# A backbone kernel on one core: first fold group in whole fp32, mod rows gathered, context modulated on VectorE

## The chip, the core and the metric

The kernel runs on one core of a Trainium2 chip. A core has five engines with queues of their own: TensorE (PE in the profile; PEld is its weight load), VectorE (DVE), ScalarE (ACT), GpSimd (POOL) and SyncE (SP), which here issues nearly all DMA transfers. Each engine works through its queue in order; semaphores make it wait for others. The metric is the device time of one execution in microseconds (us). Before the change it is 1301.46 us, the median of three runs (1300.69 to 1303.47).

## What is computed

Two layers over 1024 latent tokens of width 1024, with 256 context tokens. The parts that the change touches are the modulated norms of x and of the context, the context's projection in layer 0, and the weights of layer 1's pooling mixer:

```python
def rmsnorm(x, g):
    y = xf * lax.rsqrt(jnp.mean(xf * xf, axis=-1, keepdims=True) + RMS_EPS)
    return y * g
...
for l in range(DEPTH):
    shift, scale, gate = jnp.split(silu(c) @ mod_w[l] + mod_b[l], 3, axis=-1)
    hx = rmsnorm(x, norm_g[l]) * (1 + scale) + shift
    if l % 2 == 0:
        hc = rmsnorm(ctx, norm_g[l]) * (1 + scale_c) + shift_c
        xb_c = hc @ w_in[:, 3 * W_CONV:3 * W_CONV + W_LRU]
        _, h_ctx = rglru_branch(xb_c, pe, h0, False)
        out_x, _ = even_mixer(hx, h_ctx, pe)
    else:
        out_x = odd_mixer(hx, po, True)
    x = x + gate[:, None] * out_x
```

In the even mixer hx is multiplied by w_in (parts va, vg, ga, xb, gb); xb goes through a short convolution and a gated linear recurrence. In the odd mixer each of four groups of channels is pooled and multiplied by its `w_grp`. The kernel multiplies part of the input weights by `w_grp` beforehand: this product is called the fold.

## The kernel before

Everything is held with channels on the 128 partitions and tokens along the free axis: x in eight tiles of 128x1024 (`x_0` to `x_7`), each the tokens of 128 channels. Matmuls are made exact enough by a split: an fp32 tensor is cast to a high part of type fp32r (names with h: `h0h`, `wh_xb`, `gh`, `cth`) by ACT, and the low part, the difference (`h0l`, `wl_xb`, `gl`, `ctl`), is subtracted by POOL or DVE. Three matmul passes follow, high by high, high by low and low by high (`mm3_steps`, lines 137 to 139).

The first stage lies in `sequence` (lines 522 to 585), before the projections of layer 0 begin. It has these parts.

- **Fold** (`fold_early`, lines 296 to 334). Three groups are done here, with 4, 4 and 2 blocks of `wu`. A block of 128x1024 gives eight products of 128x512 (line 323); ACT copies the two results from PSUM (`fo`, line 328) and they are stored (`wfold`). Only the first block of group 0 is multiplied as whole fp32 (`graw` and `wu`); all others go through the split, line 101 or 106 on ACT, and four subtractions of 256 columns each on POOL (`split_small`, line 108).
- **Factors** (`dots`, line 394). A tile `mod` is multiplied on DVE with the broadcast vector `c` and summed (`junk`, line 397); ACT adds the bias (line 401) or makes the scale (`factor`, line 392). The last channels' factors come from `mod_row` (line 414): 16 matmuls on PE (line 422), a copy of the row by ACT (`modrow`, line 425), and four transposes on PE (line 428), for each of the two rows.
- **Norm of x** (`x_load`, line 459; `x_roots`, line 507). Squares on ACT, added up on POOL and DVE in `ssq`; column sums by PE (`ms_x`, line 512), root on ACT, reciprocal and a diagonal (`dg_x`, line 516) on DVE, and a matmul with ones that spreads the result over all partitions (line 519). `modulate` (line 435) then makes `h0h` and `h0l` of each tile.
- **Context** (`ctx_load`, `ctx_scale`, `ctx_split`, lines 491 to 505). The squares of eight pieces of 256 columns are added by POOL into `ssqc` (line 381); PE sums them over the channels (`ms_c`, line 194), ACT and DVE make the reciprocal root, DVE scales (line 501), POOL modulates eight pieces (line 452), ACT casts and POOL subtracts.
- **First projection** (line 825 on). The weights `xb0` are loaded and split, `wl_xb` on POOL. PE computes `xb` (48 matmuls of 512 columns), the context's `xbc` (24 of 256), `vg`, `va`, and then the gates `g` of the recurrence, which need `uc` (the short convolution of xb and xbc) and u on DVE.

The order on each engine is fixed when the program is built. Within the first stage a scheduler sets it: an instruction goes where its operands and its priority put it, `tc.high_priority` moves a step ahead, and `tc.issue_after` puts it behind another instruction. All loads of the stage form one chain on SP (`load`, line 112), so that they are issued in the order of the code. From the projections on, the order is recorded by `on` (line 595). Tiles come from rings of buffers (`wr`, `wh`, `wl`: two each; `x`: eight; `d`: 16): a new tile waits until the buffer's former one has been read for the last time.

## Time and profile before

| | |
|---|---|
| median of 3 runs | 1301.46 us (1300.69 to 1303.47) |
| profiled execution, its own time | 1300.71 us |
| span of that execution, first to last instruction | 1298.9 us |
| mean granted TensorE clock | 0.994 of full |
| DVE, ACT and POOL busy in the span | 1129.6, 660.2 and 398.5 us |
| data moved | 182.92 MB in 83507 packets |

In the rows of the timeline the columns are the start in us from the span's beginning, the length, the engine, the line, the operation, output<-input, the shape and how many instructions the row gathers; in brackets stands how long the engine was idle before and for whom it waited. In the rows of the windows they are the window, its length, for each engine the busy time and the number of instructions, the granted clock, the share of the DMA engines and GB/s. A row of waits gives who waited for whom, the sum, how often and the longest. A row of the chain that ended last gives start, length and what ran. A matmul in whole fp32 leaves two records, one in fp32r a single one.

### The profile page before, as it was taken

The numbers are of one execution on the slowest core, as the hardware profiler recorded it, in microseconds if no ns is written. First come the engines' busy times: TensorE is split into PE (matmuls) and PEld (weight loads), VectorE is DVE, ScalarE is ACT, GpSimd is POOL, SyncE is SP. The second block draws the span as 40 slices with busy tenths as digits, with TensorE's granted clock in tenths as the row PEclk, the third lists the DMA queues.
The fourth block names the chain that finished last, engine by engine and source line by source line (L and its number), as shares of the span: only waits on it lengthen the run. The fifth ranks groups of instructions, "written<-read, shape, count | busy, mean of one in ns | idle before, by whom it ended". The sixth has DMA issues, their size and how long they took to land.

```text
span 1298.9 us, 16083 instructions
## 1 busy us (share of the span) xinstructions
PE 1267.6 (98%) x5706; PEld 1039.7 (80%) x5706; DVE 1129.6 (87%) x1758; ACT 660.2 (51%) x977; POOL 398.5 (31%) x260
## 2 busy tenths in 40 slices
PE   8988999999999999999999999999999999999997
PEld 5667788888888888888888787888888888778786
DVE  7755999999999999998679868989999986887876
ACT  7663456656665654324635445744434444544543
POOL 4685347664766642353320006000000000000002
PEclk9989999999999999999999999999999999999999
DMA  9973112111221223452464555243343324677723
GB/s 371 326 221 138 49 41 73 51 56 42 73 70 55 68 77 104 140 171 98 137 200 157 188 185 179 90 147 118 111 141 132 122 99 149 228 261 251 283 98 130
DMA packets 83507, 182.92 MB, mean 141 GB/s; under 512 B 8034, under 2 KB 28002, under 8 KB 83428
## 3 DMA queue, kind: packets, MB, share of 16 engines
q1 hardware_dynamic: 76948, 178.75, 40.5%
q10 hardware_dynamic: 6480, 3.15, 0.9%
q8 instruction: 44, 0.72, 0.2%
q14 instruction: 35, 0.29, 0.1%
HBM read 137.84 MB, written 44.04 MB: 140 GB/s over the span
## 4 chain that ended last, share of the span: by engine, by line
PE 82%; DVE 7%; DMA 5%; ACT 3%; issue 1%; POOL 1%; SPq 0%; POOLq 0%; ACTq 0%; DVEq 0%
PE wob L595 7%; PE gb L595 7%; PE vg L595 6%; PE xb L595 6%; PE va L595 6%; PE g L595 4%; PE fold L323 2%; PE fold L595 2%; DMA yr_b<-y_b 2%; PE ga L595 2%; PE ga L139 2%; PE ga L137 2%; PE ga L138 2%; PE qb_v L1083 1%; PE qb_v L1085 1%; PE qb_v L1086 1%
## 5 line engine op out<-in xcount | busy, mean ns | idle before, releaser
L595 DVE SCALAR_TENSOR_TENSOR conv<-u,sm,conv 128x505 f32<-128x505 f32 (+6 forms) x224 | 153.7, 745 | 0.9
L1914 POOL TENSOR_TENSOR o<-x,rr 128x256 f32<-128x256 f32 (+1 forms) x10 | 9.4, 969 | 446.6 <-ACT rr L1850 444.7
L595 POOL TENSOR_TENSOR l<-l,l 128x1280 f32<-128x1280 f32 (+1 forms) x23 | 63.9, 2794 | 91.8 <-DVE l L595 65.6
L595 ACT ACTIVATE l<-g,sm 128x512 f32<-128x512 f32 (+1 forms) x96 | 58.6, 618 | 62.0 <-PE g L595 60.2
L595 PE MATMUL va<-h0h,wl_va 128*128 128x512 f32 x128 | 49.9, 390 | 1.3 <-POOL wl_va L595 1.3
L595 PE MATMUL vg<-h0h,wl_vg 128*128 128x512 f32 x128 | 50.0, 391 | 0.0
L595 PE MATMUL wob<-ybh,wh_wob 128*128 128x512 f32 x128 | 49.9, 390 | 0.0
L595 PE MATMUL vg<-h0h,wh_vg 128*128 128x512 f32 x128 | 49.8, 389 | 0.0
L595 PE MATMUL vg<-h0l,wh_vg 128*128 128x512 f32 x128 | 49.8, 389 | 0.0
L595 PE MATMUL wob<-ybh,wl_wob 128*128 128x512 f32 x128 | 49.8, 389 | 0.0
L595 PE MATMUL gb<-h0l,wh_gb 128*128 128x512 f32 x128 | 49.8, 389 | 0.0
L595 PE MATMUL gb<-h0h,wh_gb 128*128 128x512 f32 x128 | 49.8, 389 | 0.0
L595 PE MATMUL wob<-ybl,wh_wob 128*128 128x512 f32 x128 | 49.8, 389 | 0.0
L595 PE MATMUL va<-h0h,wh_va 128*128 128x512 f32 x128 | 49.8, 389 | 0.0
L595 PE MATMUL gb<-h0h,wl_gb 128*128 128x512 f32 x128 | 49.8, 389 | 0.0
L595 PE MATMUL va<-h0l,wh_va 128*128 128x512 f32 x128 | 49.8, 389 | 0.0
L595 DVE TENSOR_TENSOR_SCAN l<-l,l 128x256 f32<-128x256 f32 (+1 forms) x32 | 48.7, 1521 | 1.1
L101 ACT CAST wq_g<-wr_g 128x512 fp32r<-128x512 f32 x48 | 28.2, 620 | 40.8 <-DMA wr_g<-wg 15.7
L595 POOL TENSOR_TENSOR l<-l,uc 128x1280 f32<-128x1280 f32 x16 | 48.1, 3032 | 0.0
L595 DVE SCALAR_TENSOR_TENSOR conv<-cL,wsum,conv 128x506 f32<-128x506 f32 (+3 forms) x70 | 47.5, 745 | 0.2
L101 ACT CAST wq_wo<-wr_wo 128x512 fp32r<-128x512 f32 x48 | 28.7, 620 | 36.5 <-DMA wr_wo<-wo 17.3
L108 POOL TENSOR_TENSOR wl_wu<-wr_wu,wh_wu 128x256 fp32r<-128x256 f32 x24 | 17.3, 754 | 92.1 <-ACT wh_wu L106 92.1
(667 smaller groups left out, 4413.2 us busy)
## 6 DMA issues: line engine op xcount, KB each, us to landing
mod<-modT SPq DMA_DIRECT2D x20, 512.0 KB, 7.0
x_part<-xp SPq DMA_DIRECT2D x32, 256.0 KB, 3.3
mod<-modT SPq DMA_DIRECT2D x32, 256.0 KB, 3.3
wr_v<-wfold SPq DMA_DIRECT2D x16, 512.0 KB, 3.8
wr_g<-wg SPq DMA_DIRECT2D x16, 512.0 KB, 4.7
wr_wo<-wo SPq DMA_DIRECT2D x16, 512.0 KB, 3.6
y_b<-y SPq DMA_DIRECT2D x24, 256.0 KB, 3.3
y_t<-y SPq DMA_DIRECT2D x24, 256.0 KB, 3.6
```

Source lines behind the costliest of these rows:

```text
L101: return (nc.scalar.copy(hi, src), eng.tensor_tensor(out=lo, in0=src, in1=hi.bitcast(F32), op=sub))
L108: nc.gpsimd.tensor_tensor(out=lo[:, n : n + C], in0=src[:, n : n + C], in1=hi.bitcast(F32)[:, n : n + C], op=sub)
L137: nc.tensor.matmul(ps, hi[:, kc], xh[k][:, cols], start=(k == 0), stop=False)
L138: nc.tensor.matmul(ps, hi[:, kc], xl[k][:, cols], start=False, stop=False)
L139: nc.tensor.matmul(ps, lo[:, kc], xh[k][:, cols], start=False, stop=(k == ks - 1))
L323: nc.tensor.matmul(ps[s], parts[p][0][:, kc], parts[p][1][i], start=(p + i == 0), stop=(p == n - 1 and i == 3))
L595: last[eng] = f(*args, **kw)
L1083: nc.tensor.matmul(ps, hi, xh[k], start=(first and k == 0), stop=False, skip_group_check=not first)
L1085: nc.tensor.matmul(ps, hi, xl[k], start=False, stop=False, skip_group_check=not first)
L1086: mm = nc.tensor.matmul(ps, lo, xh[k], start=False, stop=(k == KH - 1), skip_group_check=not first)
L1914: nc.gpsimd.tensor_tensor(out=outs[k // per][:, k % per], in0=x1[k][:, cols], in1=rr, op=mult)
```

## The change

Nothing of the result changes but the rounding of group 0's fold. The parts are these.

- Group 0 of the fold is multiplied whole: `graw_0_*` and its four `wu` stay fp32, without casts or subtractions, 32 products in place of 8 whole ones and 72 passes. The first loads are now graw, wu, graw, mod (before: mod, graw, graw, wu).
- The ACT steps of the first factors are held back in `small_steps` until the last square of x; `decay_rates` gets a high priority. The last sum for the norm of x is on DVE.
- `mod_row`, called twice, becomes `mod_rows`: all four loads, then 32 matmul records behind the second spread matmul, one copy for both rows, the transposes. Tiles `mod` 1, 9, 2 and 10 are loaded earlier, `mod` 3 later.
- Fold group 1 follows the mod rows; the modulation of x starts earlier in the code.
- The weights `xb0` are loaded and split ahead of the context and of fold group 2. In the queues of PE, group 2 now stands between `xb` and `xbc`.
- The context's squares are added in PSUM (`csum`) by DVE, the sum is spread by one matmul, and DVE multiplies each of the eight pieces by its factor and the reciprocal root in one step and subtracts for the low part; ACT casts in between. POOL does nothing for the context.

The core of the diff:

```diff
-    def fold_early(g, kps, out_tile, g_tile):
+    def fold_early(g, kps, out_tile, g_tile, whole_tile):
         gs, gh, gl = [], [], []
         for i in range(2):
-            raw = (dtile if g < 2 else xtile)(f"graw_{g}_{i}")
+            raw = (whole_tile if g < 2 else xtile)(f"graw_{g}_{i}")
             load(raw, grp[g, i])
-            th, tl = g_tile(i)
-            split_small(raw, th, tl)
-            for t, l in ((raw, gs), (th, gh), (tl, gl)):
-                l += [t[:, h] for h in HALF]
+            if g:
+                th, tl = g_tile(i)
+                split_small(raw, th, tl)
+                for t, l in ((th, gh), (tl, gl)):
+                    l += [t[:, h] for h in HALF]
+            else:
+                gs += [raw[:, h] for h in HALF]
+                if i == 0:
+                    w0 = wpool.tile([P, D], F32, tag="wr", name="wu_0_0")
+                    load(w0, wu[0, 0])
         yield
         for kp in kps:
-            w = (dtile if (g, kp) < (1, 3) else xtile if (g, kp) == (2, 0) else wr_tile)(f"wu_{g}_{kp}")
-            load(w, wu[g, kp])
-            if (g, kp) == (0, 0):
+            if g == 0:
+                w = w0 if kp == 0 else wpool.tile([P, D], F32, tag=("wh", "wl", "wr")[kp - 1], name=f"wu_{g}_{kp}")
+                if kp:
+                    load(w, wu[g, kp])
                 parts = ((w, gs),)
             else:
+                w = (wr_tile if g < 2 else xtile)(f"wu_{g}_{kp}")
+                load(w, wu[g, kp])
                 wh, wl = [wpool.tile([P, D], F32R, tag=t, name=f"{t}_wu_{g}_{kp}") for t in ("wh", "wl")]
-                if (g, kp) == (0, 1):
-                    split(w, wh, wl, nc.vector)
-                else:
-                    split_small(w, wh, wl)
+                split_small(w, wh, wl)
...
             nc.scalar.activation(a0[:, :, k], m0[:, :, KT + k], AF.Identity, scale=col(O_NG + k), bias=bias)
 
-        def dots(m):
+        small_steps = []
+
+        def dots(m, held=False):
...
+            if held:
+                small_steps.append(step)
+            else:
+                step()
...
+        def mod_rows():
+            whole = psum("modr")
+            raws = {}
+            for j in (1, 0):
+                for q in range(KT // KW):
+                    raws[j, q] = dtile(f"modw_{j}_{q}")
+                    load(raws[j, q][:, : KW * KR * P], modW[j, q])
+            for j in (1, 0):
+                ps = whole[:2, j * KR * P : (j + 1) * KR * P]
+                with tc.issue_after(spread[0].ins):
+                    for k in range(KT):
+                        e = k % KW
+                        nc.tensor.matmul(ps, ccv[:, k], raws[j, k // KW][:, e * KR * P : (e + 1) * KR * P],
+                                         start=(k == 0), stop=(k == KT - 1))
+            row = ttile("modrow")[:2]
+            with tc.high_priority(offset=EVAC):
+                nc.scalar.copy(row, whole[:2])
+            for j in (1, 0):
+                pst = whole[:, j * KR * P : j * KR * P + 2 * KR].rearrange("p (c m) -> p m c", c=2)
+                with tc.high_priority(offset=EVAC):
+                    for e in range(KR):
+                        mm = nc.tensor.matmul(pst[:, e], row[:, (j * KR + e) * P : (j * KR + e + 1) * P], idx[:2, :2], start=True,
+                                              stop=True)
...
-        def modulate_ctx(k):
-            i, q4 = k // 4, k % 4
-            cs = slice(q4 * C, (q4 + 1) * C)
-            nc.gpsimd.tensor_scalar(out=cx[i][:, cs], in0=cx[i][:, cs], scalar1=a0[:, 1, k : k + 1],
-                                    scalar2=m0[:, 1, k : k + 1], op0=mult, op1=add)
-            ch.append(cth[i][:, cs])
-            cl.append(ctl[i][:, cs])
-            if q4 == 3:
-                last_cast[0] = split(cx[i], cth[i], ctl[i], nc.gpsimd)[0]
...
+            if i == 0:
+                csum.append(psum("csum"))
+            with tc.issue_after(high_[0].ins):
+                for q4 in range(4):
+                    v = cx[i][:, q4 * C : (q4 + 1) * C]
+                    if i + q4 == 0:
+                        nc.scalar.activation(csum[0][:, :C], v, AF.Square)
+                    else:
+                        q = ttile(f"csq_{i}_{q4}")[:, :C]
+                        nc.scalar.activation(q, v, AF.Square)
+                        nc.vector.tensor_tensor(out=csum[0][:, :C] if i + q4 < 4 else accc, in0=csum[0][:, :C], in1=q, op=add)
+
+        csum = []
 
         def ctx_scale():
-            rstd(accc, eps_r, "c")
-            for i in range(2):
-                v = cx[i].rearrange("p (k n) -> p k n", n=C)
-                nc.vector.tensor_tensor(out=v, in0=v, in1=accc.unsqueeze(1).to_broadcast([P, 4, C]), op=mult)
-
-        def ctx_split(i):
-            for k in range(4 * i, 4 * i + 4):
-                modulate_ctx(k)
+            ps, rt = csum[0][:, C : 2 * C], ttile("sq_c")[:, :C]
+            nc.tensor.matmul(ps, ones, accc, start=True, stop=True)
+            nc.scalar.activation(rt, ps, AF.Sqrt, bias=eps_r)
+            nc.vector.reciprocal(accc, rt)
+            for k in range(KT):
+                i, q4 = k // 4, k % 4
+                cs = slice(q4 * C, (q4 + 1) * C)
+                v, th, tl = [t[:, cs] for t in (cx[i], cth[i], ctl[i])]
+                shift = m0[:, 1, k : k + 1]
+                nc.vector.scalar_tensor_tensor(out=v, in0=v, scalar=a0[:, 1, k : k + 1], in1=accc, op0=mult, op1=mult)
+                nc.scalar.activation(th, v, AF.Identity, bias=shift)
+                nc.vector.scalar_tensor_tensor(out=tl, in0=v, scalar=shift, in1=th.bitcast(F32), op0=add, op1=sub)
+                ch.append(th)
+                cl.append(tl)
...
-            nc.tensor.matmul(ps, ones, t, start=True, stop=True)
+            spread[0] = nc.tensor.matmul(ps, ones, t, start=True, stop=True)
...
+        fold_some(1)
         load_mod(0)
-        fold_some(2)
+        fold_some(1)
         load(sm[:, NL:], small[:, NL:])
...
         load(idx, ident)
+        with tc.issue_after(squared[0].ins):
+            for step in small_steps:
+                step()
         with tc.high_priority(offset=EVAC):
             rx = [x_roots(h) for h in range(2)]
-        mod_row(1)
-        load_mod(2)
-        dots(2)
-        mod_row(0)
-        load_mod(KT + 2)
-        dots(KT + 2)
+        load_mod(3)
+        dots(3)
+        rows_ = mod_rows()
         fold_some(1)
+        with tc.issue_after(rows_.ins):
+            fold_some(1)
+        load_mod(KT + 3)
+        dots(KT + 3)
+        modulate(0)
+        modulate(1)
+        modulate(2)
+        modulation(4)
+        fold_some(1)
+        modulate(3)
+        fold_store()
+        modulation(5)
+        modulate(4)
         fold_some(1)
         fold_store()
-        modulation(4)
-        fold_some(1)
-        modulate(0)
-        modulation(3)
-        fold_some(1)
-        fold_store()
-        modulation(5)
-        modulate(1)
-        modulate(2)
-        modulate(3)
-        modulate(4)
         modulate(5)
         modulate(6)
         modulate(7)
-        fold_some(3)
-        fold_store()
         fold_some(1)
+        wxb = wload(win[3 * KT], "xb0", nc.gpsimd)
         ctx_load(0)
         ctx_load(1)
         nc.scalar.copy(cL, cps[0])
         fold_store()
-        ctx_scale()
-        ctx_split(0)
-        ctx_split(1)
+        fold_some(2)
+        fold_store()
+        fold_some(1)
+        with tc.high_priority(offset=EVAC):
+            ctx_scale()
...
-        w = wload(win[3 * KT], "xb0", nc.gpsimd)
+        w = wxb
```

PE at the end of group 0 (`fold_3_1` is its last result) and around the mod rows (`modr`), before:

```order
L323 MATMUL fold_3_1_414<-gh_1_206,wl_wu_3_407 128x512
L512 MATMUL ms_x_454<-ones,ssq_157 128x1 x4
L512 MATMUL ms_x_465<-ones,ssq_158 128x1 x4
L422 MATMUL modr_476<-modw_0_477,ccv 2x256 x4
L422 MATMUL modr_476<-modw_1_483,ccv 2x256 x4
L422 MATMUL modr_502<-modw_0_503,ccv 2x256 x4
L422 MATMUL modr_502<-modw_1_509,ccv 2x256
L519 MATMUL ms_x_454<-dg_x_462,ones 128x512
L519 MATMUL ms_x_465<-dg_x_473,ones 128x512
L422 MATMUL modr_502<-modw_1_509,ccv 2x256 x3
L428 MATMUL modr_476<-idx,modrow_489 128x2 x2
L428 MATMUL modr_502<-idx,modrow_515 128x2 x2
```

and now:

```order
L329 MATMUL fold_3_1_350<-graw_1_197,wu_3_347 128x512 x2
L547 MATMUL ms_x_384<-ones,ssq_157 128x1 x4
L547 MATMUL ms_x_395<-ones,ssq_158 128x1 x4
L554 MATMUL ms_x_384<-dg_x_392,ones 128x512
L554 MATMUL ms_x_395<-dg_x_403,ones 128x512
L442 MATMUL modr<-modw_0_412,ccv 2x256 x4
L442 MATMUL modr<-modw_1_414,ccv 2x256 x4
L442 MATMUL modr<-modw_0_416,ccv 2x256 x4
L442 MATMUL modr<-modw_1_418,ccv 2x256 x4
L451 MATMUL modr<-idx,modrow 128x2 x4
L329 MATMUL fold_0_0_471<-cth_136,wh_wu_0_464 128x512 x2
```

The spread matmuls (`ms_x<-dg_x`) stood behind 13 of the 16 products of the mod rows and now stand ahead of all of them, and the transposes (`modr<-idx`) come directly ahead of fold group 1 with one copied row.

POOL from the last split of fold group 1 (`wl_wu_3`) to the second weights of vg, before:

```order
L108 TENSOR_TENSOR wl_wu_3_748<-wu_3_745,wh_wu_3_747 128x256 x4
L108 TENSOR_TENSOR gl_0_789<-graw_0_786,gh_0_788 128x256 x4
L108 TENSOR_TENSOR gl_1_798<-graw_1_795,gh_1_797 128x256 x4
L108 TENSOR_TENSOR wl_wu_0_807<-wu_0_804,wh_wu_0_806 128x256 x4
L108 TENSOR_TENSOR wl_wu_1_850<-wu_1_847,wh_wu_1_849 128x256 x4
L381 TENSOR_TENSOR ssqc<-ssqc,csq_1_890 128x256
L381 TENSOR_TENSOR ssqc<-ssqc,csq_2_893 128x256
...
L381 TENSOR_TENSOR ssqc<-ssqc,csq_2_906 128x256
L102 TENSOR_TENSOR wl_xb_962<-wr_xb_959,wh_xb_961 128x1024
L381 TENSOR_TENSOR ssqc<-ssqc,csq_3_909 128x256
L102 TENSOR_TENSOR wl_vg_1042<-wr_vg_1039,wh_vg_1041 128x1024
L452 TENSOR_SCALAR cx_155<-cx_155,a_130,m_129 128x256 x4
```

and now:

```order
L108 TENSOR_TENSOR wl_wu_3_665<-wu_3_662,wh_wu_3_664 128x256 x4
L102 TENSOR_TENSOR wl_xb_706<-wr_xb_703,wh_xb_705 128x1024
L108 TENSOR_TENSOR gl_0_740<-graw_0_737,gh_0_739 128x256 x4
L108 TENSOR_TENSOR gl_1_749<-graw_1_746,gh_1_748 128x256 x4
L108 TENSOR_TENSOR wl_wu_0_758<-wu_0_755,wh_wu_0_757 128x256 x4
L108 TENSOR_TENSOR wl_wu_1_801<-wu_1_798,wh_wu_1_800 128x256 x4
L102 TENSOR_TENSOR wl_vg_969<-wr_vg_966,wh_vg_968 128x1024
L640 TENSOR_TENSOR wl_va_1010<-wr_va_1007,wh_va_1009 128x1024
```

`wl_xb` moved ahead of group 2's `gl` and `wl_wu`, and the context's sums (`ssqc`) and scaling (`cx`) are gone from between.

PE from fold group 2 (here `fold_0` and `fold_1` with `gh` and `gl`) to the context's projection `xbc`, before:

```order
L323 MATMUL fold_1_1_857<-gh_1_797,wl_wu_1_850 128x512 x2
L137 MATMUL xb_966<-h0h_636,wh_xb_961 128x512
L138 MATMUL xb_966<-h0l_637,wh_xb_961 128x512
...
L137 MATMUL xb_966<-h0h_741,wh_xb_961 128x512
L138 MATMUL xb_966<-h0l_742,wh_xb_961 128x512
L194 MATMUL ms_c<-ssqc,ones 128x256
L139 MATMUL xb_966<-h0h_741,wl_xb_962 128x512
...
L137 MATMUL xbc_965<-cth_136,wh_xb_961 128x256
L595 MATMUL vg_0_1050<-h0h_636,wh_vg_1041 128x512
L595 MATMUL vg_0_1050<-h0l_637,wh_vg_1041 128x512
```

and now:

```order
L139 MATMUL xb_893<-h0h_597,wl_xb_706 128x512
L137 MATMUL xb_893<-h0h_646,wh_xb_705 128x512
L528 MATMUL csum<-ssqc,ones 128x256
L329 MATMUL fold_0_0_764<-gh_0_739,wh_wu_0_757 128x512 x2
...
L139 MATMUL xb_893<-h0h_658,wl_xb_706 128x512
L329 MATMUL fold_1_0_807<-gh_0_739,wh_wu_1_800 128x512 x2
...
L329 MATMUL fold_1_1_808<-gh_0_739,wl_wu_1_801 128x512
L137 MATMUL xbc_892<-cth_136,wh_xb_705 128x256
L138 MATMUL xbc_892<-ctl_138,wh_xb_705 128x256
L329 MATMUL fold_1_0_807<-gh_1_748,wl_wu_1_801 128x512
L329 MATMUL fold_1_1_808<-gh_1_748,wl_wu_1_801 128x512
```

Before, group 2 was done ahead of `xb`, the context's sum (`ms_c`) stood inside `xb`, and `xbc` behind `xb`, with 33 rows of `vg` behind its first matmul. Now `xb` comes first; the sum (`csum`) stands behind 40 of its 48 matmuls, group 2 fills the place between the sum and `xbc`, and all of `xbc` comes ahead of `vg`.

More of the change, by code (lines that the diff above doesn't have):

```diff
@@ L358, in g_pair, with whole_tile @@
             return lambda i: (cth[i], ctl[i]) if g == 1 else [g_tile(f"g{n}_{g}_{i}") for n in "hl"]
[L360 removed]
+        def whole_tile(name):
+            return gpool.tile([P, D], F32, tag="g", name=name)
+        folds = (u for g in range(3) for u in fold_early(g, EARLY[g], fo_tile, g_pair(g), whole_tile))
         def fold_some(n):
@@ L412, in body @@
         ccv = spool.tile([P, KT, 2], F32, name="ccv")
[L414 to L433 removed]
+        def mod_rows():
[21 more added lines that the diff above has]
+                                              stop=True)
+                    for e in range(KR):
+                        m = j * KT + KD + e
+                        nc.scalar.activation(m0[:, :, m], pst[:, e], AF.Identity, scale=1.0 / D, bias=col(O_MB + m))
+                        if j:
+                            factor(KD + e, col(O_NG + KD + e))
+            return mm
@@ L441, in modulate @@
             th, tl = dtile(f"h0h_{k}", F32R), dtile(f"h0l_{k}", F32R)
-            nc.scalar.activation(th, t, AF.Identity, bias=shift)
+            with tc.high_priority(offset=EVAC):
+                high_[0] = nc.scalar.activation(th, t, AF.Identity, bias=shift)
             nc.vector.scalar_tensor_tensor(out=tl, in0=t, scalar=shift, in1=th.bitcast(F32), op0=add, op1=sub)
```

65 lines of the change are left out of this document (25 added, 40 removed).

## Prediction

> **What bounds the kernel now.** First the page's head, then the windows of the trace cut at places where PE (TensorE) changes its task. The profiled execution took 1300.71 us.
>
> ```profile
> span 1298.9 us, 16083 instructions
> ...
> PE 1267.6 (98%) x5706; PEld 1039.7 (80%) x5706; DVE 1129.6 (87%) x1758; ACT 660.2 (51%) x977; POOL 398.5 (31%) x260
> ```
>
> ```profile
> 9.00:13.20 4.20, 4.20 (x5) 1.81 (x6) 4.06 (x7) 2.74 (x4) 3.31 (x5) 1.00 1.02 408
> ...
> 38.40:50.30 11.90, 11.90 (x61) 6.01 (x59) 7.17 (x13) 7.33 (x15) 4.95 (x8) 1.00 1.06 400
> 50.30:73.00 22.70, 22.25 (x98) 18.07 (x98) 22.53 (x33) 17.14 (x28) 20.89 (x25) 1.00 0.86 273
> 73.00:84.90 11.90, 11.54 (x49) 8.64 (x47) 10.69 (x12) 10.11 (x17) 11.74 (x12) 1.00 0.78 236
> 84.90:157.00 72.10, 62.10 (x278) 50.85 (x279) 43.71 (x58) 21.37 (x30) 31.70 (x23) 0.93 0.31 99
> 157.00:1298.90 1141.90, 1128.12 (x5123) 935.09 (x5121) 1017.14 (x1580) 578.22 (x843) 308.82 (x169) 1.00 0.39 129
> ```
>
> The span is 1298.9 us, so 1.8 us of the profiled time lie around it. From 157.00 us on PE is busy for 1128.12 of 1141.90 us, and the order of the work from there on is the same in both programs. So what the change is worth is the shift of the matmul that starts at 157.00. Ahead of it the loss sits in one window, 84.90 to 157.00: 10.0 us of it idle, and a granted clock of 0.93. The waits of PE in the first 157 us say for whom, the chain of what ended last says how they hang together:
>
> ```profile
> PE xb L139 <- POOL wl_xb L102: 4.3, 1, 4.3
> PE fold L323 <- ACT wh_wu L101: 2.6, 1, 2.6
> PE g L595 <- DVE u L595: 2.2, 1, 2.2
> PE xbc L137 <- ACT cth L101: 2.1, 1, 2.1
> PE fold L323 <- DMA wu<-wu: 1.7, 1, 1.7
> PE va L595 <- POOL wl_va L595: 1.3, 1, 1.3
> ```
>
> ```profile
> 101.52 3.07 POOL cx L452 x4
> 104.62 1.05 ACT cth L101
> 105.72 0.39 PE xbc L137
> ...
> 116.45 0.57 ACT uc L595
> ...
> 122.31 15.28 DVE l L595 x16
> ```
>
> The second weights (wl_xb) come late, so does the context (cth), and the late context pushes the chain uc, l, u on DVE, for which PE waits again.
>
> **The change, by stages of PE.** Time of a stage is from the start of its first matmul to the start of the next stage's.
>
> ```profile
> 6.66 0.62 PE L488 MATMUL c<-ctl,ones_r 1*128 1x512 f32 x1
> 8.99 4.49 PE L323 MATMUL fold<-graw,wu 128*128 128x512 f32 x5 [1.71 <-DMA wu<-wu]
> ...
> 12.54 5.67 PE L323 MATMUL fold<-graw,wu 128*128 128x512 f32 x12
> ...
> 26.39 1.07 PE L323 MATMUL fold<-gh,wh_wu 128*128 128x512 f32 x4
> 27.30 1.07 PE L323 MATMUL fold<-gl,wh_wu 128*128 128x512 f32 x4
> 38.42 1.84 PE L512 MATMUL ms_x<-ones,ssq 128*128 128x1 f32 x16
> ```
>
> *A, first matmul of fold 0: −1.9.* It starts at 8.99, when wu, the fourth big load, has landed. A load is 0.524 MB, at 408 GB/s 1.28 us. Now wu is second, two loads earlier: about 6.4. PE is free behind the last c row, about 7.1; that decides.
>
> *B, fold 0: −0.3.* It takes 38.42 − 8.99 = 29.4 us now, 3.4 of it in two waits for casts (2.6 above, the other 0.8 by the same view). Eight of its 32 products are whole fp32 already; the 24 others were three fp32r passes of (27.30 − 26.39)/4 = 0.2275 us. A whole product is two records. The first five records take about 0.85 us each, the later ones 0.429 ((18.20 − 13.26)/11.5), so 0.858 a product: 24 × 0.858 − 72 × 0.2275 = +4.2 us of PE work, against the 3.4 of waits gone and less slow start. In full: 32 × 0.858 = 27.5. The slow start costs 0.43 a record: 5 records cost 2.1 now, and PE idled 1.7 us just before; without that idle I take 1.7 (bounds 0 to 4: none, or slow as long as 13.2 us). That is 29.1 to 29.2, −0.3. The casts and POOL subtractions of two graw and two wu leave; loads of wu come every few us against 6.9 us of work on each, so they stay hidden.
>
> The Trainium skill ("FP8 and Floating Point Precision", section TensorE Precision Notes) has true fp32 take four passes through the array. By that a product is 4 × 0.2275 = 0.91 us and fold 0 would be 1.7 us longer; the records here give 0.858, and the sum goes by them.
>
> *C, norm and mod rows: +3.0.*
>
> ```profile
> 45.90 1.98 PE L519 MATMUL ms_x<-dg_x,ones 128*128 128x512 f32 x4
> ...
> 39.48 1.28 ACT L513 ACT_TABLE_LOAD   x1
> ...
> 41.34 1.29 DVE L516 TENSOR_TENSOR dg_x<-idx,rc_x 128x512 f32<-128x512 f32 x2
> ...
> 49.36 0.36 ACT L425 COPY modrow<-modr 2x256 f32<-2x256 f32 x1 [1.90 <-PE modr L422]
> ```
>
> Now PE runs 26 mod-row records while ACT and DVE work out the norm, and never waits (11.90 busy of 11.90). After, the mod rows are ordered behind the second spread matmul. So from the end of ms_x (40.26) to the first dg_x (41.34 + 0.65) nothing is left for PE: some 1.5 us. Behind the last mod row stands one copy for both rows (0.36, with the way there and back some 0.9), then the four transposes, now without other work between: 0.6 more. Sum +3.0; bounds 0 (something else fits) and +4.5 (a copy queued behind another 1.2 us step of ACT). x and the modulated tiles come earlier, since spread does.
>
> *D, fold 1: −0.3.* 22.70 us with one wait of 0.45 for an fo copy; its splits on POOL have lost the fold 0 ones. Bounds −0.5 and +1.5 (its wl halves late by two 0.75 us subtractions).
>
> *E, from the end of fold 1 to 157.00: −16.2.*
>
> ```profile
> 132.11 0.28 PE L595 MATMUL xbc<-cth,wh_xb 128*128 128x256 f32 x1
> 132.23 0.28 PE L595 MATMUL xbc<-ctl,wh_xb 128*128 128x256 f32 x1
> ...
> 157.00 0.39 PE L595 MATMUL vg<-h0h,wh_vg 128*128 128x512 f32 x1
> ```
>
> The stretch takes 84.0 us. Its work: five times 48 matmuls of 512 columns (fold 2, xb, vg, va, the next xb) at 0.2275 = 54.6; 48 of 256 at 0.12 = 5.8; gates 24 and 12 of these = 6.9; 0.4 for the context's sum. That is 67.7, so 16.3 are lost: the four waits above 9.9, with about 0.16 of drain each; 20 matmuls at 0.43 instead of 0.23 behind two of the waits, 4.0 (the clock of 0.93 above); the rest, 1.8, in short gaps. I keep 0.1 (a drain at vg). What takes the place of each:
>
> ```profile
> 64.09 2.85 POOL L108 TENSOR_TENSOR wl_wu<-wu,wh_wu 128x256 fp32r<-128x256 f32 x4 [1.24 <-ACT wh_wu L106]
> ...
> 80.05 7.55 POOL L381 TENSOR_TENSOR ssqc<-ssqc,csq 128x256 f32<-128x256 f32 x6
> 87.55 2.34 POOL L102 TENSOR_TENSOR wl_xb<-wr_xb,wh_xb 128x1024 fp32r<-128x1024 f32 x1
> ...
> 119.12 2.38 POOL L595 TENSOR_TENSOR wl_va<-wr_va,wh_va 128x1024 fp32r<-128x1024 f32 x1 [7.68 <-ACT wh_va L595]
> ...
> 98.41 1.75 DVE L197 RECIPROCAL ssqc<-sq_c 128x256 f32<-128x256 f32 x1 [13.81 <-ACT sq_c L196]
> ...
> 77.50 2.06 DVE L439 SCALAR_TENSOR_TENSOR x<-x,a,ms_x 128x512 f32<-128x512 f32 x3
> ```
>
> The weights' low half wl_xb (2.34) leaves its place behind the squares' sums (7.55) and fold 2's splits on POOL and stands right behind fold 1's last split, which ends at 66.9 now: ready between 69.3 and, 3 us later with stage C's delay, 72.4, against a need near 73.8 (its third matmul, 73.3 being the end of D). Slack 1.4 at least. The context's sum stands behind 40 of xb's 48 matmuls (9.1 us, 82.4). Then the sum 0.4, root 0.5, reciprocal 1.75, sixteen DVE steps of half the 0.69 us that a 512-column one takes (5.5; at a whole 0.69 11.0), with ACT's first cast between (1.05): ready at 91.6 to 97.1. xbc now stands behind the last 8 of xb and 44 of fold 2, 11.8 us behind the sum, about 94.6. So slack is 3 at the likely end and −2.5 at the other; I take the near end, by the nearest row. wl_va waits for ACT's cast wh_va (the 7.68 us of its row), whose buffer xb's weights hold until xbc is done; xbc now ends 48 vg matmuls, 10.9 us, ahead of va, and cast and split take 1.05 + 2.38: hidden by 7. The tightest is wl_vg: its buffer is free with fold 2's last matmul, near 95.0; cast and split end 3.4 later, 98.4, and PE wants it behind the rest of xbc (2.9) and two matmuls, 98.4. Slack 0. And u: the chain from xbc's end (just before uc, 116.45) through DVE to u ended 22 us later, for which PE had 15 of vg, 48 of va and 24 of xbc, 17.2 us; xbc now stands ahead of all of vg, so 96 and 24 lie between, 24.7 us. Slack 2.7. Where a wait is gone, the slow clock behind it goes too.
>
> The steps that I cost at nothing: the last x sum on DVE (0.70), held factors and decay_rates early, under fold 0's 27 us on DVE and ACT; without that cover some 1 us each. mod loads earlier: the queue of loads is full until 70 us, but none of the products waits for it.
>
> **Sum:** −1.9 − 0.3 + 3.0 − 0.3 − 16.2 = −15.7, that is 1285.0 on the profiled execution's own 1300.71. The median of the runs shown (1301.46) is 0.75 above it; I forecast 1285.5.
>
> **Rivals.**
> *One wait comes back in E (0.20).* The context late by 2.5, or DVE's chain to u by as much. Two of the four idles were followed by 12 and 8 matmuls at the slow clock, 2.4 and 1.6 us more. Total 2 to 5: 1287.5 to 1290.5. For it: slacks of 0 to 3 us are thin in a stretch of 84. Against it: each rests on a step taken at its longest.
>
> ```profile
> 83.31 1.28 DVE L443 SCALAR_TENSOR_TENSOR h0l<-x,m,h0h 128x1024 fp32r<-128x1024 f32 x1 [0.45 <-ACT h0h L442]
> ...
> 52.16 1.92 DVE L443 SCALAR_TENSOR_TENSOR h0l<-x,m,h0h 128x1024 fp32r<-128x1024 f32 x1
> ```
>
> The step takes 1.92 beside POOL's subtractions of weights, 1.28 beside its sums of squares. If all 16 context steps pay 0.5 to 0.65 beside fold 2's splits, the context is ready 8 to 10 us later, xbc waits 5 to 7, and with a slow clock behind it the time is 1293 (chance 0.07). The Trainium skill ("SBUF — State Buffer", section Who interferes with whom) states it as a rule: a DVE instruction with two SBUF inputs and a GpSimd one that reads SBUF exclude each other for a whole instruction. It speaks against moving the context to DVE; by that rule the 1.92 agrees.
>
> *Mod rows cost nothing and no slow start (0.13):* 1281 to 1283.5.
>
> *The slow side (0.03).* Fold 0 runs at the half rate of its first five records throughout: 32 × 0.85 = 27 us, less the 1.7 counted, 1311. It decides from 18 slow products (15.7/0.85) on. Against it: from 13.2 us on the records of before run at 0.429 while PE stays busy, and nothing else in fold 0 differs. The Trainium skill ("TensorE: Matmul & The Clock Gate", section What's actually happening) lets the rate rise after one busy window of 3.413 us; by that the slow start ends after 2 to 4 products, 1.7 to 3.4 us, inside B's bounds.
>
> *It does not do what it says (0.01):* the order of both programs shows wl_xb and the context where the change puts them.
>
> **How the numbers follow.** Forecast (1283.5 to 1287.5) 0.56, a wait back 0.20, better 0.13, context far late 0.07, slow 0.04 with the last. The range 1281 to 1291 leaves out the last two and some edges. 0.2% (2.6 us) is about what a measurement of this kernel can tell from none: faster by more 0.95, within 0.02, slower 0.03.
>
> **What would show it.** The vg matmul of 157.00 near 141.3; fold 0 from about 7 to 36; a hole of 1.5 us ahead of the spread; no wait over 1 us for wl_xb, cth, wl_va or u; granted clock 1.00 in all windows behind fold 0. A wait of 2 us at xbc or the gates, or a hole in fold 0 for a load, would make it wrong.

## The result and the profile after

The changed kernel takes 1288.01 us (1287.69 to 1288.91, four runs), the kernel before 1301.76 (1300.69 to 1303.47, four runs, those shown ahead among them): a ratio of 0.9894, 95% interval 0.9877 to 0.9911. That is 13.75 us, where 15.7 were forecast.

The head of the page after, with the span and the busy time of each engine:

```profile
span 1285.6 us, 16024 instructions
...
PE 1268.5 (99%) x5682; PEld 1033.6 (80%) x5682; DVE 1131.9 (88%) x1779; ACT 655.8 (51%) x977; POOL 369.8 (29%) x226
```

Now PE's waits in the first 160 us (engine and tile that waits, who ends it; us in total, times, longest):

```profile
PE ms_x L554 <- DVE rc_x L549: 1.6, 1, 1.6
PE busy L492 <- DVE tiny L162: 1.1, 1, 1.1
PE modr L451 <- ACT modrow L446: 0.7, 1, 0.7
PE c L505 <- ACT cth L101: 0.5, 1, 0.5
PE modr L451 <- ACT m L455: 0.5, 1, 0.5
PE fold L329 <- ACT fo L334: 0.5, 1, 0.5
```

All of the waits that bounded the kernel before are gone: the 4.3 us for wl_xb, 2.6 for a cast, 2.2 for u, 2.1 for the context, 1.7 for a load, 1.3 for wl_va. In their place stand the 1.6 us hole ahead of the spread matmul and two waits for the copy of the mod rows, 0.7 and 0.5. The windows of the trace, cut by what PE does now (us, then busy time and count of PE, its weight loads, DVE, ACT and POOL, then granted clock, DMA share, GB/s):

```profile
9.00:36.00 27.00, 27.00 (x61) 11.85 (x60) 22.10 (x48) 15.09 (x32) 7.65 (x6) 1.00 1.03 409
36.00:50.00 14.00, 11.75 (x55) 5.41 (x53) 11.80 (x19) 9.02 (x12) 6.53 (x8) 1.00 0.97 373
50.00:73.00 23.00, 22.02 (x92) 17.78 (x93) 22.33 (x32) 15.12 (x26) 15.75 (x18) 0.93 0.72 216
73.00:142.00 69.00, 69.00 (x333) 58.07 (x332) 51.45 (x77) 31.37 (x51) 28.91 (x23) 1.00 0.49 169
142.00:1285.00 1143.00, 1131.29 (x5131) 935.93 (x5129) 1019.13 (x1585) 577.45 (x844) 310.74 (x170) 1.00 0.39 129
```

In 73 to 142, the stretch that lost 16 us before, PE is busy for 69.00 of 69.00 us at a granted clock of 1.00. The clock is below one only in 50 to 73, fold 1 (0.93). The timeline of PE gives the starts of the stages (start, duration of the group):

```profile
7.20 29.92 PE L329 MATMUL fold<-graw,wu 128*128 128x512 f32 x64
36.96 1.84 PE L547 MATMUL ms_x<-ones,ssq 128*128 128x1 f32 x16
40.40 1.95 PE L554 MATMUL ms_x<-dg_x,ones 128*128 128x512 f32 x4 [1.60 <-DVE rc_x L549]
42.29 7.07 PE L442 MATMUL modr<-modw,ccv 128*2 128x256 f32 x32
50.02 0.60 PE L451 MATMUL modr<-idx,modrow 2*128 2x2 f32 x4 [0.66 <-ACT modrow L446]
51.13 0.60 PE L451 MATMUL modr<-idx,modrow 2*128 2x2 f32 x4 [0.51 <-ACT m L455]
51.66 1.34 PE L329 MATMUL fold<-cth,wh_wu 128*128 128x512 f32 x4
52.80 1.91 PE L329 MATMUL fold<-ctl,wh_wu 128*128 128x512 f32 x4
...
55.78 1.19 PE L329 MATMUL fold<-cth,wh_wu 128*128 128x512 f32 x4
56.81 1.08 PE L329 MATMUL fold<-ctl,wh_wu 128*128 128x512 f32 x4
...
75.94 0.39 PE L137 MATMUL xb<-h0h,wh_xb 128*128 128x512 f32 x1
...
143.71 0.39 PE L640 MATMUL vg<-h0h,wh_vg 128*128 128x512 f32 x1
```

The vg matmul that started at 157.00 starts at 143.71. From it to the end of the span both kernels take 1141.9 us, so those 13.3 us are the whole difference of the spans (1298.9 and 1285.6). By stage, each from its first matmul to the next stage's, in us:

| stage | before | after | difference | forecast |
|---|---|---|---|---|
| A, up to the first fold matmul | 8.99 | 7.20 | −1.8 | −1.9 |
| B, fold 0 | 29.43 | 29.76 | +0.3 | −0.3 |
| C, norm and mod rows (up to 51.66) | 11.88 | 14.70 | +2.8 | +3.0 |
| D, fold 1 (up to 75.94) | 22.67 | 24.28 | +1.6 | −0.3 |
| E, to the vg matmul | 84.03 | 67.77 | −16.3 | −16.2 |
| sum | 157.00 | 143.71 | −13.3 | −15.7 |

So the missing 2.4 us lie in D (1.9) and B (0.6). In D the fold rows from 52.80 on come four in 1.70 us (52.80 to 54.50), 0.426 each, and from 56.81 at the usual pace. Cut into pieces of 3.4 us (same columns as above), the trace shows it in the clock:

```profile
49.40:52.80 3.40, 2.27 (x13) 1.92 (x14) 3.40 (x6) 2.11 (x9) 3.40 (x5) 0.97 0.02 10
52.80:56.20 3.40, 3.40 (x10) 2.69 (x9) 3.37 (x6) 2.39 (x3) 2.56 (x5) 0.53 0.31 35
56.20:59.60 3.40, 2.95 (x14) 2.12 (x13) 3.33 (x6) 0.77 (x2) 2.67 (x3) 1.00 0.83 274
```

PE was busy for only 2.27 of 3.40 us around the copy, 1.2 of them in eight transposes of 2x2, and the next 3.4 us ran at 0.53. Eight matmuls at 0.426 in place of 0.2275 cost 1.6 us. That this pause is what slowed the clock was a reading at this point; the experiments below test it.

The thin covers of stage E can be read from DVE's timeline after:

```profile
86.14 1.75 DVE L530 RECIPROCAL ssqc<-sq_c 128x256 f32<-128x256 f32 x1 [5.75 <-ACT sq_c L529]
87.94 3.26 DVE L536 SCALAR_TENSOR_TENSOR cx<-cx,a,ssqc 128x256 f32<-128x256 f32 x8
91.11 2.86 DVE L538 SCALAR_TENSOR_TENSOR ctl<-cx,m,cth 128x256 fp32r<-128x256 f32 x7
94.19 0.66 DVE L538 SCALAR_TENSOR_TENSOR ctl<-cx,m,cth 128x256 fp32r<-128x256 f32 x1 [0.22 <-ACT cth L537]
...
126.06 1.28 DVE L640 TENSOR_TENSOR u<-va,sg 128x512 f32<-128x512 f32 x2
```

The context is split by 94.85 and xbc starts at 97.27: 2.4 us of slack, where 3 were forecast. The first u is done at 126.70 and the next 512-column gate starts at 126.81: hidden, with nothing to spare where 2.7 were forecast. Contrary to what stands ahead, the gates do not read u: in the code they multiply the halves of uc (`uh`, `ul`), while u reads the PSUM tile of va. So what PE waited for before, as far as the code tells, is a PSUM buffer that u releases.

### The profile page after: what moved, and what is told of

Read it like the earlier page. It is cut to its first block, busy times and chain, and to the rows that moved or that the text cites. A ratio compares the mean times of both kernels' runs of the same rounds, so it can differ in the third digit from the quotient of the medians.

```text
span 1285.6 us, 16024 instructions
## 1 busy us (share of the span) xinstructions
PE 1268.5 (99%) x5682; PEld 1033.6 (80%) x5682; DVE 1131.9 (88%) x1779; ACT 655.8 (51%) x977; POOL 369.8 (29%) x226
## 4 chain that ended last, share of the span: by engine, by line
PE 73%; DVE 13%; DMA 8%; issue 3%; ACT 2%; POOL 1%; SPq 0%; POOLq 0%; ACTq 0%; DVEq 0%
PE vg L640 7%; PE wob L640 7%; PE gb L640 7%; PE va L640 7%; PE xb L640 6%; PE fold L329 5%; PE g L640 4%; PE ga L640 2%; PE xbc L640 2%; DMA x_part<-xp 1%; PE qb_g L1128 1%; PE qb_g L1131 1%; PE qb_g L1130 1%; PE qb_v L1131 1%; PE qb_v L1130 1%
## 5 line engine op out<-in xcount | busy, mean ns | idle before, releaser
L101 ACT CAST wq_v<-wr_v 128x512 fp32r<-128x512 f32 x48 | 28.2, 620 | 50.5 <-DMA wr_v<-wfold 19.8
```

What stands on the lines that cost most here:

```text
L101: return (nc.scalar.copy(hi, src), eng.tensor_tensor(out=lo, in0=src, in1=hi.bitcast(F32), op=sub))
```

## The experiments

Each ran beside the kernel before on the same chip. Span minus the start of the vg matmul was 1139.2 to 1143.2 us over all traces, so two kernels less than some 3 us apart can't be told apart by their times; the place of the vg matmul in the trace is given with them. That place is of one execution, and a slow stretch of the clock, which moves it by some 1.6 us, does not fall alike in all of them. Times are medians, with the range, the ratio to before and its interval.

### What the two halves are worth

**The second half alone (late_half):** before, with the weights xb0 ahead and the context summed in PSUM and modulated by DVE; fold 0 split, mod rows and first loads as before.

```diff
...
-        fold_some(3)
+        fold_some(1)
+        wxb = wload(win[3 * KT], "xb0", nc.gpsimd)
+        fold_some(2)
...
-        ctx_scale()
-        ctx_split(0)
-        ctx_split(1)
+        with tc.high_priority(offset=EVAC):
+            ctx_scale()
```

> The kernel before with the second half of the change alone: the weights xb0 ahead of fold group 2, and the context's squares, scaling and low parts on DVE; fold 0, the factors and the mod rows stay as before, so x is modulated some 5 us later than in the changed kernel. Theory 1 (the gain of 16 us lies in these two parts, and the first half of the change only costs): vg starts at 141 to 144, time 1284 to 1288. Theory 2 (they need x early: DVE comes to the context only after h0l, near 85 us, and the context's chain of 9 us then has only 4 us of xb to hide in): xbc waits 3 to 5 us, the gates wait for u as before, vg at 148 to 152, time 1292 to 1297.

1290.75 us (1287.56 to 1292.19), 0.9899 [0.9870, 0.9928]; vg at 147.48, 9.5 us ahead of 157.00. The waits for wl_xb and at xbc are gone. What is left of the large ones in E, in PE's waits of this kernel:

```profile
PE g L615 <- DVE u L615: 2.2, 1, 2.2
```

The place of vg lies between those of the two theories. By it 9.5 of the 13.3 us come from the second half; the ratio alone (0.9899) can't be told from the changed kernel's 0.9894. The other 3.8 need the first half as well: xb starts 0.9 earlier here (75.05), but the stretch from there to vg takes 72.4 us in place of 67.8, with the 2.2 us wait for u, and 1.6 more in the 3.4 us at half rate that follow it (129.19 to 132.61). What the first half brings, by the traces, is an earlier x: DVE begins on it at 41.54 after and at 47.06 here, and the context's sum is done at 80.4 and 88.5. That the missing wait at the gates comes from this was not tested by itself.

**Fold 0 whole, alone (fp32_alone):** before, with group 0 multiplied in fp32 and no casts or subtractions for it.

```diff
...
-            if (g, kp) == (0, 0):
+            if g == 0:
                 parts = ((w, gs),)
...
-                if (g, kp) == (0, 1):
-                    split(w, wh, wl, nc.vector)
-                else:
-                    split_small(w, wh, wl)
+                split_small(w, wh, wl)
```

> The kernel before with one thing changed: group 0 of the fold in whole fp32, loads in their old order. Theory 1 (whole fp32 trades 3.4 us of waits for 4.2 us of work): fold 0 takes 28.5 to 30.5 us against 29.43, vg starts at 156 to 158, time within 1.5 of before. Theory 2 (freed POOL and ACT bring the later splits forward): vg at 153 to 155, time 1297 to 1299.

1303.97 us (1299.19 to 1307.12, ten runs) against 1299.97, 1.0024 [1.0012, 1.0036]; vg at 159.58, 2.6 later. Fold 0 takes 29.16 us, 0.3 less than before, as the sum for B said; but what stands behind it lost, by PE's waits of this kernel:

```profile
PE xbc L137 <- ACT cth L101: 6.2, 1, 6.2
PE xb L139 <- POOL wl_xb L102: 2.6, 1, 2.6
```

The wait for the context is 6.2 us in place of 2.1. POOL ends the context's last sum at 94.3 in place of 90.6. By itself the whole fold gains nothing, and slightly loses: the first theory's fold, but a later vg and a longer time than either theory gave.

**The first weights ahead, alone (xb_early_alone):** before, with only the weights xb0 ahead, as in late_half.

```diff
-        fold_some(3)
+        fold_some(1)
+        wxb = wload(win[3 * KT], "xb0", nc.gpsimd)
+        fold_some(2)
...
-        w = wload(win[3 * KT], "xb0", nc.gpsimd)
+        w = wxb
```

> The kernel before with one thing changed: the weights xb0 are loaded and split ahead of group 2 of the fold; the context stays with POOL. Theory 1 (the place of the weights brings its own 6.7 us): the wait for wl_xb and the slow window behind it go, time 1294 to 1296. Theory 2 (the wait moves to the context or to fold 2's low parts, which POOL now does later): xbc or fold 2 waits 3 us or more, time 1298 to 1302.

1297.38 us (1292.61 to 1298.65, ten runs) against 1300.78, 0.9965 [0.9950, 0.9979]; vg at 151.36, 5.6 earlier. The median lies between the two theories' ranges, and the profiled execution (1294.12) is one of the fastest of the ten. The 4.3 us for wl_xb are gone with their slow clock; the rest of the chain still waits:

```profile
PE xbc L137 <- ACT cth L101: 2.5, 1, 2.5
...
PE g L597 <- DVE u L597: 2.2, 1, 2.2
```

### Parts of the change undone

**Weights back at their old place (xb_late):** the changed kernel, fold 2 ahead of xb again.

```diff
-        wxb = wload(win[3 * KT], "xb0", nc.gpsimd)
...
-        w = wxb
+        w = wload(win[3 * KT], "xb0", nc.gpsimd)
```

> The changed kernel with the weights xb0 loaded and split at the old place, behind fold group 2, whose matmuls then stand ahead of xb on PE again. Theory 1 (their place was worth the 4.3 us wait and the slow clock behind it, 6.7 us): PE waits 3 to 5 us between fold 2's splits and wl_xb, a slow window follows, time 1293 to 1296. Theory 2 (the context's sums were what held POOL, and they are on DVE now): waits of 0 to 2 us, time 1288 to 1290.

1291.83 us (1290.64 to 1293.99), 0.9932 [0.9908, 0.9956]; vg at 146.83, 3.1 later than after. That lies between the two theories, and by a third way: the weights are not waited for even here. Fold 2, next in line, waits for its own cast, and the context comes just too late:

```profile
PE fold L329 <- ACT wh_wu L106: 2.2, 1, 2.2
...
PE xbc L138 <- DVE ctl L538: 0.4, 1, 0.4
```

What the early weights give in the changed kernel is work for PE (xb) while fold 2's casts are made.

**The context back on POOL (ctx_pool):** the changed kernel with DVE scaling by the root in two steps, and POOL modulating and splitting.

```diff
-                nc.vector.scalar_tensor_tensor(out=v, in0=v, scalar=a0[:, 1, k : k + 1], in1=accc, op0=mult, op1=mult)
-                nc.scalar.activation(th, v, AF.Identity, bias=shift)
-                nc.vector.scalar_tensor_tensor(out=tl, in0=v, scalar=shift, in1=th.bitcast(F32), op0=add, op1=sub)
...
+                nc.gpsimd.tensor_scalar(out=v, in0=v, scalar1=a0[:, 1, k : k + 1], scalar2=shift, op0=mult, op1=add)
...
+                if q4 == 3:
+                    split(cx[i], cth[i], ctl[i], nc.gpsimd)
```

> The changed kernel with the context scaled on DVE in two steps, modulated by POOL in eight (0.77 us each) and subtracted by POOL in two (2.4 each), as before, at the new place behind csum. Theory 1 (the move to DVE is needed): POOL has 11 us of context work beside fold 2's splits, ctl comes 5 to 8 us after its need at 97.4 or fold 2's second block waits, time 1292 to 1297. Theory 2 (fold 2 between the sum and xbc hides it on either engine): time 1288 within 1.

1291.64 us (1290.00 to 1293.21), 0.9932 [0.9915, 0.9948]; vg at 146.51, 2.8 later. The wait comes back at xbc, and at the weights that POOL splits behind the context:

```profile
PE xbc L138 <- POOL ctl L102: 1.2, 2, 0.7
...
PE vg L643 <- POOL wl_vg L102: 0.8, 1, 0.8
```

The mechanism is the first theory's, its size just below that theory's range.

**Fold 0 split again (fold_split):** the changed kernel with group 0 cast and subtracted as before.

```diff
...
-            if g:
-                th, tl = g_tile(i)
-                split_small(raw, th, tl)
...
+            th, tl = g_tile(i)
+            split_small(raw, th, tl)
...
-                split_small(w, wh, wl)
+                if (g, kp) == (0, 1):
+                    split(w, wh, wl, nc.vector)
+                else:
+                    split_small(w, wh, wl)
```

> The changed kernel with group 0 of the fold split again in high and low parts (one block whole, three in three passes), its raw tiles in the d ring. Theory 1 (whole fp32 costs 4.2 us of PE and saves 3.4 us of waits): fold 0 takes 28.5 to 30 us against 29.76, time 1287.3 to 1288.5, no difference that can be told. Theory 2 (the split is what held PE up, and whole fp32 brings much of the gain): time 1290 to 1292. Theory 3 (whole fp32 is a pure cost now that loads are reordered): 1284 to 1285.

1288.15 us (1287.09 to 1291.92), 0.9902 [0.9885, 0.9919]: no difference to the changed kernel in time, as the first theory said. The profiled execution is the slowest of the four (1291.92, vg at 148.00) and shows what can go wrong with the split: a wait for a cast, a longer hole ahead of the spread.

```profile
PE fold L329 <- ACT wh_wu L106: 2.7, 1, 2.7
PE ms_x L554 <- DVE rc_x L549: 2.6, 1, 2.6
```

### The slow clock in fold 1

**Fold 1 no longer behind the mod rows (rows_free):**

```diff
-        with tc.issue_after(rows_.ins):
-            fold_some(1)
+        fold_some(1)
```

> One line less than the changed kernel: fold group 1 need not wait for the transposes of the mod rows, so its first products fill the place where PE waits for the row's copy. Theory 1 (the idle 1.2 us at the copy, with the tiny transposes, brings one window of slow clock over fold 1): no slow window, fold 1 back to 22.5 to 23 us from 24.28, xb starts near 73.2 instead of 75.94, time 1285.0 to 1285.8 against 1288.0. Theory 2 (fold 1 is slow for a reason of its own): the slow records stay, only the idle 1.2 us go, time near 1286.8.

1287.14 us (1286.54 to 1287.98), 0.9898 [0.9883, 0.9912]; vg at 145.27. Fold 1 starts at 48.87, ahead of the copy, but so early that it waits for POOL's split:

```profile
PE fold L329 <- POOL wl_wu L108: 0.7, 3, 0.3
```

The slow rows come back at 55.4 to 58.4. The hole moved, the clock with it; neither theory holds in full.

**Mod rows no longer behind the spread (spread_free):** the `with tc.issue_after(spread[0].ins):` over the products of `mod_rows` taken away.

> The changed kernel with the mod rows free to run ahead of the spread matmuls, as before the change. Theory 1 (the 1.6 us hole ahead of the spread was the price of getting x earlier): the hole closes, 14.7 us from ms_x to fold 1 become 13.1, but x is modulated 4 to 5 us later, and the low parts of h0, done 3.9 us ahead of their need now, come 1 us late: time 1286.5 to 1288. Theory 2 (x had room enough): 1286.4 or less and no wait of xb for h0l. The gap at the copy stays in both, and with it the slow clock over fold 1.

1289.45 us (1286.78 to 1290.99), 0.9913 [0.9894, 0.9932]; vg at 144.02. The hole ahead of the spread is gone, the two at the copy grew from 0.7 and 0.5 to 1.1 and 0.7 (ACT is at an h0h until 48.06, with the last mod row done at 47.46); C takes 14.13 in place of 14.70 and the slow rows stay (51.6 to 54.6). xb waits for no h0l, as the second theory said, but the time is above both ranges.

**ACT's casts of fold 1 ahead of the first h0h (cast_first), and this with rows_free (cast_rows):**

```diff
...
-        nc.scalar.copy(hi, src)
+        whole_cast[0] = nc.scalar.copy(hi, src)
...
+                if k == 0:
+                    mctx.enter_context(tc.issue_after(whole_cast[0].ins))
```

> The changed kernel with only the two casts moved ahead of the first h0h; fold 1 still stands behind the transposes. Theory 1 (idle time of PE in one window of some 3.4 us brings the slow clock): the 1.2 us at the copy stay, so does the slow window, fold 1 takes 24 us as in the changed kernel, xb starts at 75.3 to 76. Theory 2 (late low parts are what fold 1 loses by): fold 1 takes 22.7, xb starts at 73.5 to 74.5.

> rows_free, and ACT casts the second cth and the first wh_wu of fold group 1 ahead of the first h0h, which waits for DVE anyway. In rows_free the hole only moved: fold 1 waited for POOL's low parts of wu instead of the copy, and the slow clock came all the same. Theory 1 (POOL's splits start 2 to 3 us late because ACT stands waiting for x): fold 1 starts near 49 and runs without a hole or a slow window, xb starts at 71.5 to 73 against 75.94 in the changed kernel, vg at 139.5 to 141 against 143.71, time 1284 to 1285.5. Theory 2 (the low parts of x or the chain to u are the next bound): a wait of 1 to 3 us in xb or at the gates, vg at 141.5 to 143, time 1286 to 1287.5.

cast_first: 1287.35 us (1286.46 to 1291.43), 0.9900 [0.9877, 0.9922], vg at 143.97, slow rows as in the changed kernel, as the first theory said. cast_rows: 1286.89 us (1283.69 to 1291.38, six runs), 0.9894 [0.9872, 0.9915]; its profiled execution (1289.89, vg at 146.37, later than either theory gave) has no slow window in fold 1, but one at the hole ahead of the spread:

```profile
36.00:50.00 14.00, 12.40 (x45) 5.44 (x44) 10.85 (x18) 8.80 (x12) 8.68 (x11) 0.76 0.96 361
50.00:73.00 23.00, 21.98 (x96) 15.62 (x95) 20.14 (x30) 12.45 (x25) 9.52 (x14) 1.00 0.62 176
```

The same 1.60 us hole stands in the changed kernel's trace, with four spread matmuls in 1.95 us behind it. Here they took:

```profile
41.05 3.75 PE L559 MATMUL ms_x<-dg_x,ones 128*128 128x512 f32 x4 [1.60 <-DVE rc_x L554]
```

Seven of the traces have this hole of 1.60 us, and only this one is slow there. So one and the same hole brings a slow window in one execution and none in another.

**Eight of the mod rows' products free, with cast_rows (half_rows):**

```diff
-                with tc.issue_after(spread[0].ins):
+                with ExitStack() as rctx:
+                    if not j:
+                        rctx.enter_context(tc.issue_after(spread[0].ins))
```

> cast_rows with half of the mod rows (eight products, 3.5 us) free to fill the hole ahead of the spread, so that neither hole is left. Theory 1 (holes and the slow windows behind them are what the changed kernel still loses, and where they fall against the clock's windows is what spreads the runs): no slow window in 36 to 75 us, from ms_x to fold 1 11 to 12.5 us against 14.70, xb starts at 71.5 to 73, vg at 139.5 to 141; median 1284 to 1286, and the runs lie within 3 us, where those of cast_rows spread over 7.7. Theory 2 (x comes 1.7 us later and its low parts are the bound): xb waits, vg at 141.5 to 143.5, no gain over 1287.

1288.82 us (1286.72 to 1290.08), 0.9904 [0.9889, 0.9920]; vg at 144.84. Both holes are gone, PE is busy for 14.00 of 14.00 us from 36 to 50, and C takes 10.78, 3.9 less than after. Then fold 1 waits, and has its slow rows at 59.6 to 62.6:

```profile
PE fold L331 <- ACT fo L336: 3.2, 2, 2.5
```

No gain, as the second theory said, though not at the tile that it named: on ACT the copy `fo` stands behind a cast and an h0h, and the h0h waited 2.1 us for DVE's x (it starts at 55.12).

**The pause filled (warm):** the changed kernel with ten more 128x128 products, which nobody reads, six behind the last mod row and four between the transposes.

```diff
...
+            warm = psum("warm")
+
+            def keep(n, ins):
+                for _ in range(n):
+                    with tc.high_priority(offset=EVAC), tc.issue_after(ins):
+                        last_ = nc.tensor.matmul(warm[:, :P], ones, ones, start=True, stop=True)
+                    ins = last_.ins
+
+            keep(6, mm.ins)
...
+                    if j:
+                        keep(4, mm.ins)
```

> The changed kernel with ten dummy matmuls of 128x128 in the two holes at the mod row's copy (six behind the last mod row, four between the two halves of the transposes), into a PSUM tile that nobody reads; nothing else moves. Theory 1 (idle time at the copy brings the slow clock over fold 1): the dummies cost 0.3 to 0.6 us, the slow window is gone, fold 1 takes 22.4 to 23 us against 24.28, vg starts at 142.5 to 143. Theory 2 (the slow clock comes from something else, the 1.6 us ahead of the spread, for one): a slow window stays between 50 and 60 us, vg starts at 144 or later. The time moves by 1.2 us or less in either case, so the trace decides.

1293.52 us (1291.58 to 1296.01), 0.9946 [0.9930, 0.9963]; vg at 150.72. Windows of this kernel, the first two at the same places as those of after above:

```profile
49.40:52.80 3.40, 3.40 (x28) 3.14 (x27) 3.40 (x6) 1.81 (x6) 3.40 (x5) 1.00 0.03 13
52.80:56.20 3.40, 3.40 (x17) 2.79 (x17) 3.37 (x5) 2.66 (x5) 2.07 (x3) 1.00 0.25 28
...
69.20:72.60 3.40, 1.13 (x6) 0.63 (x4) 2.14 (x4) 1.18 (x2) 0.74 (x2) 1.00 0.98 295
72.60:76.00 3.40, 2.86 (x7) 1.79 (x8) 2.45 (x2) 3.40 (x5) 2.30 (x1) 0.53 1.10 393
76.00:79.40 3.40, 3.40 (x10) 2.64 (x9) 3.19 (x5) 3.04 (x7) 0.29 (x1) 0.50 1.05 385
```

With the pause filled, the clock in 52.80 to 56.20 is 1.00 in place of 0.53, and PE starts 17 matmuls there in place of 10. This is one execution, and cast_rows shows that executions differ; but the pause at the copy stands in six traces (after, xb_late, ctx_pool, fold_split, spread_free, cast_first), and in all six half rate follows within fold 1. So the pause was the cause. The rest of the expectation, that nothing else moves, failed. The queue of PE came out in another order, xb's first rows ahead of the last block of fold 1; there PE waited 2.3 us for wh_xb (69.2 to 72.6, busy for 1.13) and ran two windows at 0.53 and 0.50. So the price of the pause, 1.6 us, is read from the rows, and not confirmed by a time.

None of the twelve is surely faster than the changed kernel: cast_rows has the lowest single time (1283.69), but its range covers the other's.

## Why the prediction was right

The time, 1288.01, is in the range and faster by far more than 0.2%. It is 0.5 us beyond the forecast case's own 1283.5 to 1287.5 and has the number of the rival "one wait comes back in E", but not its mechanism: E has no such wait. By its own steps:

- **That the shift of the vg matmul is all:** right, 1141.9 us behind it in both.
- **A, −1.9:** right (−1.8), decided by the c rows, as said (the last at 6.65).
- **B, −0.3:** measured +0.3. The products at 0.858 us gave 32 × 0.858 = 27.5; the slow start, taken as 1.7, was 29.76 − 27.46 = 2.3. The idle of 1.7 us that was thought to lengthen it is gone, and it still covers five records. Over all traces it covers three to six, with or without that idle, so that there were five both times is chance:

```profile
7.20 4.60 PE L329 MATMUL fold<-graw,wu 128*128 128x512 f32 x5
```

- **C, +3.0:** right (+2.8), hole (1.60 of the 1.5 said) and copy included.
- **D, −0.3: this is the term that was mis-sized,** at +1.6. Its bounds ended at +1.5 and were given for late wl halves, which did not come. The prediction counted the copy for 0.9 us and the transposes for 0.6 in C and held that the clock would be 1.00 in all windows behind fold 0. It had priced slow matmuls behind 2 to 4 us waits in E, yet none behind C's own new holes. In their place the runs showed a pause of 1.1 us in 3.4, with 1.2 us of tiny transposes in it, a window at 0.53 behind it, and none when it was filled (warm).
- **E, −16.2:** right (−16.3); the work counted as 67.7 us takes 67.77. The parts behave as told when taken apart: context on POOL, a wait at xbc (ctx_pool); weights early alone, 4.3 us less at wl_xb and the rest of the chain still late (xb_early_alone). That nothing at all came back was luck in part: two of the covers held by 0.1 us or less (next point).
- **The covers:** the context's slack was near (2.4 for 3); each of its DVE steps takes 0.41 us (3.26/8), where half of 0.69 was taken. wl_vg, forecast at 0, was ready 0.06 ahead (split from 98.84 in 2.40, its first weight load at 101.30). The slack of u was off: 2.7 forecast, 0.1 measured. The chain was taken to start at xbc's end, 101.2, but ACT began uc at 104.81, having waited for a buffer that a store still read:

```profile
104.81 0.56 ACT L640 ACTIVATE uc<-xbc,sm 128x256 f32<-128x256 f32 x1 [5.23 <-DMA wfold<-fo]
```

- **Context far late, by steps slowed beside POOL:** did not come. The exclusion is there, but POOL paid: its four subtractions of 256 columns took 2.82 us at 83.19 and 5.40 at 91.44, beside the ctl steps. One of them took 3.12 in place of some 0.73, while seven ctl steps stayed at 0.41; only the eighth, behind a gap of 0.22 on DVE, took 0.66. The Trainium skill ("SBUF — State Buffer", section Who interferes with whom) leaves it to the order of issue who blocks; these rows agree with it.

```profile
83.19 2.82 POOL L108 TENSOR_TENSOR wl_wu<-wu,wh_wu 128x256 fp32r<-128x256 f32 x4
91.44 5.40 POOL L108 TENSOR_TENSOR wl_wu<-wu,wh_wu 128x256 fp32r<-128x256 f32 x4 [5.44 <-ACT cth L537]
```

- **Slow side, fold 0 at half rate throughout:** did not come; 27.00 of 27.00 us busy with 29.76 in all.

## What to carry to other kernels

A stretch with many small waits is best summed as its work alone and then checked cover by cover; here that gave 16.2 of 16.3 us, and the early work paid because it filled PE while others prepared, more than by the wait it was aimed at (xb_late). Price a new hole on TensorE with the clock behind it: a pause of 1 to 2 us can cost 1.6 us more, and very small matmuls in it do little against that. Add up what PE streams in the 3.4 us around it (next section). Parts of a change don't add: the whole fold alone was slightly slower (fp32_alone), and split again in the changed kernel it made no difference (fold_split), so each is worth what the stage behind it can use.
